# A rotary-embedding kernel on one core: tile t takes batches t, t+4, t+8 and t+12 in place of four neighbouring ones

## The chip, the core and the metric

The kernel runs on one core of a Trainium2 chip. The time is the device time of one launch in microseconds (us); the figure for the kernel before is the median of three runs. The work of this kernel lies on two resources: VectorE (DVE in the profile), which does all the arithmetic, and the 16 DMA engines of the core, which carry every tile from DRAM into SBUF and back. SyncE (SP) and GpSimd (POOL) do nothing here but start transfers. In this document one of the 16 DMA engines is called a lane.

## The reference: what is computed

The input x has 16 batches, 512 positions, 16 heads and 64 values, all float32 (33.55 MB); cos and sin are 512 x 32. Of each 64 values the first 32 are rotated in two quarters of 16, and the last 32 are passed on.

```python
x1, x2 = (x[..., :half_dim].copy(), x[..., half_dim:].copy())
...
rotated_first = x1[..., :half_dim // 2] * cos[..., :half_dim // 2] - x1[..., half_dim // 2:] * sin[..., :half_dim // 2]
rotated_second = x1[..., :half_dim // 2] * sin[..., :half_dim // 2] + x1[..., half_dim // 2:] * cos[..., :half_dim // 2]
return np.concatenate([rotated_first, rotated_second, x2], axis=-1)
```

All batches use the same cos and sin rows, so which batches share a tile does not matter to the arithmetic.

## The kernel before

**Tiles.** The 16 x 512 = 8192 positions are cut into T = 4 tiles. A tile is 128 partitions (P) of K = 16 positions each; a position is R = 1024 floats (16 heads x 64), so one partition's row is 16 x 1024 x 4 B = 64 KB and a tile is 8.39 MB. One batch of 512 positions takes PB = 32 partitions, so a tile holds four batches, one in each group of 32 partitions. Before the change a tile is one contiguous stretch of DRAM: row p of tile t starts at (128 t + p) x 64 KB.

**Buffers.** `ring` (line 45) has NS = 3 places in SBUF; tile t lives in place t % 3, so tile 3 uses the place of tile 0 again. The arithmetic is done in place, and the store reads the same buffer.

**Transfers.** `load` (line 54) and `store` (line 57) are one DMA each: 128 rows of 64 KB, or of 32 KB where tile 2 is loaded in two halves (KC = 8 positions each). On SP's queue stand, in this order: load 0, load 1, the first half of load 2 (lines 65 to 67); then store 0, the second half of load 2, load 3 (lines 107 to 109); then store 1 (line 112) and store 3 (line 126). Store 2 alone is started by POOL (line 116), after the small loads of cos and sin (lines 63 and 64). Load 3 must wait until store 0 has read the place that both use. Store 1 is held back by hand until the middle of tile 2's rotation: lines 118 to 123 make it wait for `near`, the rotation of positions 8 to 12 of tile 2, which itself waits for the second half of load 2.

**Arithmetic.** `rotate` (line 90) is four VectorE instructions for half a tile: two products and two sums (lines 96, 97, 98 and 101). Before the first of them, lines 73 to 86 spread cos and sin over the four groups of 32 partitions.

**What the change touches.** Only the two DRAM views `xf` and `of` (lines 36 and 37) and the indexing of them in `load` and `store`.

Of the kernel before, what the change touches and what calls it, by code (L numbers as in the profile page):

```python
# [1 line left out]

# [4 lines left out]


@with_exitstack
def kernel(  # L10
    ctx: ExitStack,
    tc: tile.TileContext,
    x: bass.AP,
    cos: bass.AP,
    sin: bass.AP,
    out: bass.AP,
):
    nc = tc.nc
    fp32 = mybir.dt.float32
    P = 128  # L20
    B, S, H, D = x.shape
    Q = D // 4
    HF = D // 2

    K = 16
    T = B * S // (P * K)
    PB = S // K
    REP = P // PB  # L30
    R = H * D
    NS = 3
    KC = K // 2
    KM = 13

    xf = x.rearrange("b s h d -> (b s h d)").rearrange("(t p f) -> t p f", t=T, p=P)
    of = out.rearrange("b s h d -> (b s h d)").rearrange("(t p f) -> t p f", t=T, p=P)
    cosf = cos.rearrange("(p k) j -> p (k j)", k=K)
    sinf = sin.rearrange("(p k) j -> p (k j)", k=K)

    const_pool = ctx.enter_context(tc.tile_pool(name="const", bufs=1))
    b_pool = ctx.enter_context(tc.tile_pool(name="bp", bufs=1, space=bass.MemoryType.PSUM))


    ring = const_pool.tile([P, NS, K, H, D], fp32)
    stage = const_pool.tile([P, 2, K, HF], fp32)
    spun = const_pool.tile([P, 2 * K, Q], fp32)
    packed = const_pool.tile([PB, 2 * K, Q], fp32)
    table = const_pool.tile([P, 2, K, 2, Q], fp32)

    def rows(t, lo, hi):
        return ring[:, t % NS, lo:hi].rearrange("p k h d -> p (k h d)")

    def load(t, lo=0, hi=K):
        return nc.sync.dma_start(out=rows(t, lo, hi), in_=xf[t, :, lo * R : hi * R])

    def store(t, lo=0, hi=K, queue=nc.sync):
        return queue.dma_start(out=of[t, :, lo * R : hi * R], in_=rows(t, lo, hi))  # L58


    nc.vector.memset(stage[:, :, :, 0:Q], 0.0)  # L61
    spread = stage.rearrange("(j b) t k i -> j b t (k i)", b=REP)
    nc.gpsimd.dma_start(out=spread[:, 0, 0], in_=cosf)  # L63
    nc.gpsimd.dma_start(out=spread[:, 0, 1], in_=sinf)  # L64
    load(0)
    load(1)
    load(2, 0, KC)

    PQ = PB // REP
    nc.vector.stream_shuffle(  # L73
        out=spun[:],
        in_=stage.rearrange("p t k j -> p (t k) j")[:, :, 0:Q],
        mask=[j % PQ * REP for j in range(PB)],
    )
    for q in reversed(range(REP)):
        n = PQ * (q + 1)
        nc.vector.tensor_copy(out=packed[0:n], in_=spun[q * PB : q * PB + n])  # L80

    for r in range(REP):
        nc.vector.tensor_copy(  # L83
            out=table[r * PB : (r + 1) * PB].rearrange("p t k c j -> p (t k) c j"),
            in_=packed.unsqueeze(2).to_broadcast((PB, 2 * K, 2, Q)),
        )
    C = table[:, 0].rearrange("p k c j -> p k (c j)")
    Sn = table[:, 1].rearrange("p k c j -> p k (c j)")

    def rotate(t, lo, hi):  # L90
        x1 = ring[:, t % NS, lo:hi, :, 0:HF]
        c = C[:, lo:hi].unsqueeze(2).to_broadcast((P, hi - lo, H, HF))
        s = Sn[:, lo:hi].unsqueeze(2).to_broadcast((P, hi - lo, H, HF))
        b_full = b_pool.tile([P, KC, H, HF], fp32, name="b_t")
        b_t = b_full[:, 0 : hi - lo]
        nc.vector.tensor_mul(out=b_t, in0=x1, in1=s)  # L96
        nc.vector.tensor_mul(out=x1, in0=x1, in1=c)  # L97
        nc.vector.tensor_sub(  # L98
            out=x1[:, :, :, 0:Q], in0=x1[:, :, :, 0:Q], in1=b_t[:, :, :, Q:HF]
        )  # L100
        return nc.vector.tensor_add(  # L101
            out=x1[:, :, :, Q:HF], in0=x1[:, :, :, Q:HF], in1=b_t[:, :, :, 0:Q]
        )

    rotate(0, 0, KC)
    rotate(0, KC, K)
    store(0)
    load(2, KC, K)
    load(3)
    rotate(1, 0, KC)  # L110
    rotate(1, KC, K)
    behind_loads = store(1)
    rotate(2, 0, KC)
    near = rotate(2, KC, KM)
    rotate(2, KM, K)
    store(2, queue=nc.gpsimd)

    tc.add_manual_dep(
        behind_loads.ins,
        near.ins.name,  # L120
        mybir.DependencyInfo(mybir.DependencyClass.Sync, mybir.DependencyReason.DATA),
        reason="the store follows the loads at the DMA engines",
    )
    rotate(3, 0, KC)
    rotate(3, KC, K)
    store(3)


# [1 line left out]
_INS = ['x', 'cos', 'sin']  # L130
_OUTS = [((16, 512, 16, 64), 'float32')]


# [23 lines left out]
```

## Time and profile before

| quantity | value |
|---|---|
| median of three runs | 161.63 us (161.45 to 161.63) |
| span of the profiled execution | 159.5 us |
| VectorE busy | 112.9 us in 47 instructions |
| one `rotate` of half a tile (lines 96, 97, 98, 101) | 4.43 + 4.42 + 2.29 + 2.28 us |
| first VectorE instruction on x / end of the last one | 22.99 us / about 131.2 us |
| first row of x moving / last row of the output landed | 1.74 us / 158.2 us |
| packets of 64 KB, and the time of most of them | 896; 2.418 us |
| packets of 32 KB, and the time of most of them | 256; 1.213 us |

The span is the time from the first to the last instruction of one profiled execution; the measured time of a run is some 2.1 us longer. A packet is what one lane carries in one piece; its time runs on that lane. Here each row of a tile is one packet. VectorE's last rotation ends 28 us before the span does: what follows it is the last store. The profile gives "share of 16 engines' span" for each DMA queue: the time of its packets added up and divided by 16 times the span.

### The profile page before, as it was taken

What the parts mean: (1) busy time and instruction counts of PE and PEld (TensorE: products, weight loads), DVE (VectorE), ACT (ScalarE), POOL (GpSimd) and SP (SyncE); (2) the same over time, 40 slices, a digit from 0 to 9 for tenths busy, and PEclk for the clock granted to TensorE, in tenths of its full rate; (3) what the DMA queues carried; (4) which work ended last, traced back from release to release, by engine and by line L of the source; (5) the groups of instructions that cost most, each with busy time, mean ns of one, the idle gap of its engine ahead of it and who ended that gap; (6) DMA issues with size and microseconds to landing.
All of it is one profiled execution on the core that took longest, in us unless ns stands there. A gap on an engine that the chain in (4) does not pass through costs nothing.

```text
span 159.5 us, 115 instructions
## 1 busy us (share of the span) xinstructions
DVE 112.9 (71%) x47; POOL 1.9 (1%) x7
## 2 busy tenths in 40 slices
DVE  1000959999999999999999999999999990000000
POOL 3000000000000000000000000010000000000000
DMA  7969979899699699699996996996996996998966
GB/s 263 542 263 542 444 345 526 362 427 526 271 493 551 263 526 526 263 395 427 493 526 263 526 526 263 526 526 263 526 526 263 526 510 279 526 427 362 526 263 263
DMA packets 1360, 67.24 MB, mean 422 GB/s; under 512 B 176, under 2 KB 176, under 8 KB 208
## 3 DMA queue, kind: packets, MB, share of 16 engines
q1 hardware_dynamic: 1152, 58.72, 85.7%
q0 software_dynamic: 208, 8.52, 12.4%
HBM read 33.69 MB, written 33.55 MB: 422 GB/s over the span
## 4 chain that ended last, share of the span: by engine, by line
DVE 61%; DMA 14%; issue 5%; DVEq 1%
DVE b_t L96 22%; DVE ring L97 22%; DMA ring<-in_x_dram 14%; DVE ring L101 10%; DVE ring L98 7%; DVEq L152 1%; DVEq L96 0%
## 5 line engine op out<-in xcount | busy, mean ns | idle before, releaser
L96 DVE TENSOR_TENSOR b_t<-ring,table 128x4096 f32<-128x4096 f32 (+2 forms) x9 | 35.6, 3959 | 2.1 <-DMA ring<-in_x_dram 1.9
L97 DVE TENSOR_TENSOR ring<-ring,table 128x4096 f32<-128x4096 f32 (+2 forms) x9 | 35.6, 3950 | 0.3
L98 DVE TENSOR_TENSOR ring<-ring,b_t 128x2048 f32<-128x2048 f32 (+2 forms) x9 | 18.4, 2050 | 0.3
L101 DVE TENSOR_TENSOR ring<-ring,b_t 128x2048 f32<-128x2048 f32 (+2 forms) x9 | 18.4, 2043 | 0.0
L73 DVE LOAD_MASK_SELECT spun<-stage x1 | 0.0, 14 | 14.4 <-DMA stage<-in_sin_dram 14.4
L83 DVE COPY table<-packed 32x1024 f32<-32x1024 f32 x4 | 2.7, 684 | 0.1
L58 POOL DMA_DIRECT2D out_dram<-ring x1 | 0.6, 559 | 101.7 <-DVE ring L101 101.7
L80 DVE COPY packed<-spun 32x512 f32<-32x512 f32 (+3 forms) x4 | 1.7, 416 | 0.1
L61 DVE MEMSET stage<- 128x512 f32 x1 | 0.5, 485 | 0.9 <-PEq L141 0.9
L73 DVE STREAM_SHUFFLE spun<-stage 128x512 f32<-128x512 f32 x1 | 0.7, 722 | 0.0
L63 POOL DMA_DIRECT2D stage<-in_cos_dram x1 | 0.6, 642 | 1.3 <-DVE stage L61 1.3
L64 POOL DMA_DIRECT2D stage<-in_sin_dram x1 | 0.5, 532 | 0.0
L141 POOL MEMSET const-bfloat16-1.0<- 128x1 bf16 x1 | 0.1, 101 | 0.0
L141 POOL MEMSET const-float32-0.0<- 128x1 f32 x1 | 0.1, 98 | 0.2 <-issue 0.2
L141 POOL MEMSET const-float32-1.0<- 128x1 f32 x1 | 0.1, 98 | 0.0
L141 POOL MEMSET const-uint8-127<- 128x1 uint8 x1 | 0.1, 98 | 0.0
## 6 DMA issues: line engine op xcount, KB each, us to landing
ring<-in_x_dram SPq DMA_DIRECT2D x2, 4096.0 KB, 40.7
stage<-in_cos_dram POOLq DMA_DIRECT2D x1, 64.0 KB, 8.9
stage<-in_sin_dram POOLq DMA_DIRECT2D x1, 64.0 KB, 13.3
ring<-in_x_dram SPq DMA_DIRECT2D x3, 28.9
out_dram<-ring SPq DMA_DIRECT2D x3, 27.4
out_dram<-ring POOLq DMA_DIRECT2D x1, 39.5
```

The source lines that it names most:

```text
L58: return queue.dma_start(out=of[t, :, lo * R : hi * R], in_=rows(t, lo, hi))
L61: nc.vector.memset(stage[:, :, :, 0:Q], 0.0)
L63: nc.gpsimd.dma_start(out=spread[:, 0, 0], in_=cosf)
L64: nc.gpsimd.dma_start(out=spread[:, 0, 1], in_=sinf)
L73: nc.vector.stream_shuffle(out=spun[:], in_=stage.rearrange("p t k j -> p (t k) j")[:, :, 0:Q], mask=[j % PQ * REP for j in range(PB)],)
L80: nc.vector.tensor_copy(out=packed[0:n], in_=spun[q * PB : q * PB + n])
L83: nc.vector.tensor_copy(out=table[r * PB : (r + 1) * PB].rearrange("p t k c j -> p (t k) c j"), in_=packed.unsqueeze(2).to_broadcast((PB, ...
L96: nc.vector.tensor_mul(out=b_t, in0=x1, in1=s)
L97: nc.vector.tensor_mul(out=x1, in0=x1, in1=c)
L98: nc.vector.tensor_sub(out=x1[:, :, :, 0:Q], in0=x1[:, :, :, 0:Q], in1=b_t[:, :, :, Q:HF])
L101: return nc.vector.tensor_add(out=x1[:, :, :, Q:HF], in0=x1[:, :, :, Q:HF], in1=b_t[:, :, :, 0:Q])
L152: with _tile.TileContext(nc) as tc:
```

## The change

The two DRAM views are built from the batch dimension (g t) instead of from one flat stretch: t is the inner of the two, so tile t has g = 0 to 3 at batches t, t+4, t+8 and t+12. One batch is 2 MB, so the four groups of 32 partitions of one tile are 8 MB apart in DRAM, where they were 2 MB apart. Rows stay 64 KB long and 64 KB apart within a group, and partition 32 g + j still holds positions 16 j to 16 j + 15 of its batch, so the cos and sin tables fit as before.

```diff
-    xf = x.rearrange("b s h d -> (b s h d)").rearrange("(t p f) -> t p f", t=T, p=P)
-    of = out.rearrange("b s h d -> (b s h d)").rearrange("(t p f) -> t p f", t=T, p=P)
+    xf = x.rearrange("(g t) (j k) h d -> t g j (k h d)", t=T, k=K)
+    of = out.rearrange("(g t) (j k) h d -> t g j (k h d)", t=T, k=K)
...
-        return nc.sync.dma_start(out=rows(t, lo, hi), in_=xf[t, :, lo * R : hi * R])
+        return nc.sync.dma_start(out=rows(t, lo, hi), in_=xf[t, :, :, lo * R : hi * R])
...
-        return queue.dma_start(out=of[t, :, lo * R : hi * R], in_=rows(t, lo, hi))
+        return queue.dma_start(out=of[t, :, :, lo * R : hi * R], in_=rows(t, lo, hi))
```

The DRAM side of a transfer thus has three dimensions, 4 x 32 x 16384, where it had two, 128 x 16384. The SBUF side keeps 128 partitions. In the built program the instructions of every engine stand in the same order as before, with the same waits; only the shapes in the nine large transfers differ (here SP's queue; the shape is that of the destination):

```
-L55 DMACopy ring<-in_x_dram 128x16384 x2
-L55 DMACopy ring<-in_x_dram 128x8192
-L58 DMACopy out_dram<-ring 128x16384
+L55 DMACopy ring<-in_x_dram 128x1x16384 x2
+L55 DMACopy ring<-in_x_dram 128x1x8192
+L58 DMACopy out_dram<-ring 4x32x16384
```

## The prediction

> **What bounds the kernel now.** I read the head of the page, its slices and its DMA queues first, then the DMA shares of three windows, then the waits of SP's queue, and last the chain.
>
> ```profile
> span 159.5 us, 115 instructions
> ...
> DVE 112.9 (71%) x47; POOL 1.9 (1%) x7
> ...
> DVE  1000959999999999999999999999999990000000
> ...
> DMA  7969979899699699699996996996996996998966
> ...
> DMA packets 1360, 67.24 MB, mean 422 GB/s; under 512 B 176, under 2 KB 176, under 8 KB 208
> ...
> q1 hardware_dynamic: 1152, 58.72, 85.7%
> q0 software_dynamic: 208, 8.52, 12.4%
> HBM read 33.69 MB, written 33.55 MB: 422 GB/s over the span
> ```
>
> VectorE is idle at both ends, the lanes never are: 85.7 + 12.4 = 98.1% of 16 lanes' time is packets. So the lanes set the end. In numbers: 98.1% of 16 x 159.5 us is 2503 us of lane time for 67.24 MB, 26.9 GB/s a lane. The packet records say it more sharply: of 896 packets of 64 KB nearly all took 2.418 us (27.1 GB/s), loads and stores alike, the 32 KB ones 1.213 us; 16 packets were in flight for 150.7 us, one on each lane. The windows show the same rate in the loads' stretch, in the mixed one and in the last store:
>
> ```profile
> core 0: us, DVE busy (x) POOL busy (x), PEclk, DMA share, GB/s
> 4.00:20.00 16.00, 4.01 (x9) 0.00 (x0) 1.00 1.04 451
> 72.00:99.00 27.00, 26.72 (x12) 0.00 (x0) 1.00 1.03 447
> 140.00:157.00 17.00, 0.00 (x0) 0.00 (x0) 1.00 1.00 432
> ```
>
> (A packet is counted where it starts, hence shares a little over 1.) The small packets tell how a transfer is dealt out: 176 under 512 B is 11 transfers x 16, one closing packet per lane and transfer; q1's 1152 is 8 transfers x 16 plus 5 loads' and 3 stores' 1024 rows. So now all 16 lanes take part in every transfer, 8 rows of 128 each.
>
> ```profile
> SPq L58 <- DVE ring L101: 84.1, 3, 30.5
> ...
> SPq L55 <- DMA out_dram<-ring: 21.0, 1, 21.0
> ```
>
> SP waits long, but the lanes have queued rows meanwhile; those waits cost nothing. The chain of waits names VectorE for most of the span:
>
> ```profile
> DVE 61%; DMA 14%; issue 5%; DVEq 1%
> ```
>
> It runs by semaphores and does not see rows queued on a lane; its DVE share is no sign that VectorE binds. A lower bound of the kernel is the rows' lane time: (896 x 2.418 + 256 x 1.213) / 16 = 154.8 us; 4.7 us of the span are the start (1.74 us before the first row), the slower first rows (2.9 to 3.45 us) and the tail.
>
> **The change, part by part.** *Arithmetic and order:* nothing. The same instructions stand on VectorE, with the same waits; 0 us. *Starting a transfer:* each large transfer has one dimension more. SP's issues took 0.34 us (stores) and 0.43 us (loads), POOL's of the same size 0.56 us. A form that costs as much as POOL's adds 0.2 us on each of eight SP issues; one that is simpler to set up costs nothing or saves as much. Only the first lies ahead of the first row, the others behind queued rows: 0 to 0.2 us, I take 0. *DRAM addresses:* groups lie 8 MB apart, not 2 MB. Every row now takes 2.418 us wherever it lies, so nearer or farther apart there is no time to win but the 1.2 us per lane that slow packets lost above 2.418 us; below that no gain. As a loss I know no row; it stays under the next term, since fewer rows move at once.
>
> *How the rows are dealt to lanes* is the large term. All eleven transfers of the trace have a count of 128 or 32 as outermost dimension on both sides, and all used 16 lanes. Now the nine large ones have an outermost count of 4 on the DRAM side and 128 on the SBUF side. The trace has no such transfer, so I bound it. Low end: rows are dealt by the SBUF side as now, 16 lanes, change 0. High end: one lane for each of the four outer pieces, 32 rows each. A transfer then takes 32 x 2.418 = 77.4 us instead of 8 x 2.418 = 19.3 us. I take four lanes: in every transfer of the trace a lane got whole indices of the outermost dimension (128 / 16 = 8, and 16 closing packets also for the 32 rows of cos), and of 4 there are only four to give.
>
> [...]
>
> *What the four lanes do to each other.* Lane 1 walks partitions 0 to 31, lane 2 partitions 32 to 63, and so on, in step. Low end: each runs its 2.418 us per row, as now where 16 lanes run side by side: eight whole transfers x 77.4 = 619 us. High end: the lanes meet in pairs at one path, and each row takes twice as long, 4.836 us: eight x 154.8 = 1238 us. The nearest row for streams that meet is q0 with q1: store 2 took 39.5 us to land against 27.4 us for q1's, since two streams on a lane take turns and nothing of it overlaps:
>
> ```profile
> out_dram<-ring SPq DMA_DIRECT2D x3, 27.4
> out_dram<-ring POOLq DMA_DIRECT2D x1, 39.5
> ```
>
> Also, a load's row and a store's row take the same 2.418 us though DRAM is read in one and written in the other, so the 27.1 GB/s are set by what both share, lane or SBUF's side; before, each lane had its own eight partitions, so the two were never told apart. I take the high end: lanes started within 0.43 us of each other stay in step, so whatever they share they share all the time.
>
> [...]
>
> *The schedule with T = 154.8 us a transfer.* Loads 0, 1 and half of 2 are queued at once and end at 2.5 T; store 0 is queued after tile 0's rotation (27 us, hidden under load 1) and runs to 3.5 T, half of load 2 to 4 T, load 3 (which waits for store 0, landed half a T earlier) to 5 T. Store 2 goes by POOL's queue from about 4 T on and takes turns with load 3; both end by 6 T; store 1, queued meanwhile, runs to 7 T, and store 3, whose rotation took 27 us under store 1, to 8 T. The lanes are never without rows; all of VectorE's 112.9 us lies under them. If that cover were gone, it would cost a tile's 27 us at most at the end. Sum: 8 T = 1238, + 4.7 for start and tail = 1243 us of span, + 2.1 us (161.6 - 159.5, what a run has around the span) = 1245 us against the median of 161.63.
>
> **The rivals.**
> *Four lanes at full rate.* For it: 2.418 us never changed with what else was moving. Against: no row there had lanes on each other's partitions. 619 + 4.7 + 2.1 = 626 us (own range 610 to 660).
> *Something between.* Lanes fall out of step and meet only in part of the rows (650 to 1200 us), or POOL's store 2 uses four other lanes than SP's: then SP's lanes carry seven transfers, 7 x 154.8 + 6.8 = 1090 us, or 549 at full rate. For it: POOL's transfers have their own queue. Against: in the trace q0 and q1 used the same lanes, and rows kept in step.
> *The other side: still 16 lanes, dealt by the SBUF side.* One mechanism, deciding as soon as the count of lanes is 16: then only addresses differ. For it: the SBUF side still has 128 partitions. Against: a lane would have to take a part of an outermost index, which no transfer of the trace shows. It gives 161.6 us less at most the 1.2 us that slow packets cost now: 160.4 to 161.8 us, not slower. Then the change would do nothing to the time.
>
> **How the numbers follow.** Pairs in step (1200 to 1260 us): 0.58. Four lanes at full rate (610 to 660): 0.22. Between (660 to 1200): 0.10. Store 2 apart at full rate (549): 0.03. Sixteen lanes: 0.07, of which 0.03 faster, 0.02 the same and 0.02 slower by the issue cost. The predicted time is that of the first, 1245 us. It holds 0.58 alone, so the range must take in the full-rate case: 605 to 1265 us, with 0.9 inside. About 0.2%, 0.3 us, is what a measurement here can tell from no change. Slower: 0.58 + 0.22 + 0.10 + 0.03 + 0.02 = 0.95; the same 0.02; faster 0.03.
>
> **What would show it.** Four lanes: DMA share of about 25% of 16 engines over the whole span, 4 in place of 16 closing packets for each of q1's transfers (q1's count 1056 in place of 1152), VectorE idle for four fifths of the span or more. Pairs: rows of 64 KB at about 4.84 us and some 54 GB/s; full rate: 2.42 us and 108 GB/s. A whole load landing about 155 us (77 us) after the first. Store 2 on other lanes: share above 25% while it runs. Wrong altogether: a DMA line of 7s to 9s as before, and 16 packets in flight.

## The result and the profile after

The changed kernel took 884.53 us (median of six runs, 867.69 to 893.85) against 161.63 us before: 5.38 times as long, 95% interval 5.369 to 5.388. That ratio is taken over the faster runs of the six alone; over their median it would be 5.47. The forecast of 1245 us, slower, had the direction and both causes, four lanes and pairs of them at one path; the time lies between its first two cases, since the pairs did not stay in step.

The head of the page, the slices and the queues of the changed kernel:

```profile
span 868.8 us, 115 instructions
...
DVE 112.9 (13%) x47; POOL 2.1 (0%) x7
...
DVE  0200000560000065150000006000001910000000
...
DMA  2222222222222222222222222222222222222220
GB/s 57 58 51 57 51 54 57 54 57 57 60 57 63 60 71 84 77 69 69 72 71 89 104 100 86 106 109 106 103 100 100 106 97 81 84 94 91 97 97 39
DMA packets 1648, 67.24 MB, mean 77 GB/s; under 512 B 464, under 2 KB 464, under 8 KB 496
...
q1 hardware_dynamic: 1056, 58.72, 22.2%
q0 software_dynamic: 592, 8.52, 2.5%
```

VectorE does the same 112.9 us of work. The DMA line is the new thing: a flat row of 2s where 6s to 9s stood, 22.2 + 2.5 = 24.7% of 16 lanes, that is four lanes that are never idle and twelve that carry no row of a tile. q1's packets fell from 1152 to 1056: 1024 rows and 4 closing packets for each of eight transfers. The GB/s line says the rest: about 55 in the first third, over 100 in the middle, and down and up again in the last third. The same bytes, the same four busy lanes, and two rates. The windows put numbers on it (length, busy times, clock, DMA share, GB/s):

```profile
core 0: us, DVE busy (x) POOL busy (x), PEclk, DMA share, GB/s
25.00:150.00 125.00, 5.13 (x10) 0.00 (x0) 1.00 0.25 55
170.00:300.00 130.00, 18.23 (x7) 0.00 (x0) 1.00 0.25 59
560.00:660.00 100.00, 0.00 (x0) 0.00 (x0) 1.00 0.25 104
725.00:860.00 135.00, 0.00 (x0) 0.00 (x0) 1.00 0.24 88
```

What waits now is VectorE, for the loads, and SP, for store 0 before load 3; store 2, which takes turns with load 3, lands after 169.8 us:

```profile
DVE b_t L96 <- DMA ring<-in_x_dram: 556.4, 5, 145.2
```

```profile
SPq L55 <- DMA out_dram<-ring: 190.8, 1, 190.8
```

```profile
out_dram<-ring POOLq DMA_DIRECT2D x1, 169.8
```

In the packet records most rows of 64 KB are of two kinds: 423 of 896 under 2.5 us, as before, and 321 over 4 us, most of them 4.8 to 5.13 us; the 152 between took the slow rate in part. The account of a lane is then simple, as a mean over the four and by the time at which a row starts. Rows at the old speed would fill 619.3 us of each of the four lanes. Above that they lost, per lane: 80.2 us by 161 us (load 0), 66.3 by 310 (load 1), 16.0 by 366 (half of load 2), 30.5 by 455 (store 0), 7.2 by 525 (the other half), 9.9 by 671 (load 3 beside store 2), 6.1 by 725 and 18.7 in the last stores: 234.9 us. 619.3 + 234.9 is 854.2 us of the 865.4 between the first row and the last landing; the lanes did not all end at the same time.

The pattern inside a lane shows what a slow row meets. These are the times, in us, at which the two lanes of one pair begin each group of four rows of load 0 and load 1 (the records do not name lanes; rows are strung together by one's end and the next one's start):

```
first lane   41.46  60.85  79.99  98.91  117.57  135.99  154.10  172.04  189.78
second lane  42.09  61.80  81.11  100.19 119.01  137.59  155.84  173.93  191.84
behind by     0.64   0.95   1.12    1.28    1.44    1.60    1.74    1.89    2.06
```

On the first lane three rows of a group take 4.9 to 5.04 us, and one row at the boundary is shorter, and shorter each time (4.29, 4.10, 3.93, 3.74, 3.56 us): there the first lane has gone on to the next four partitions and the second has not followed yet. On the second lane the first and the last row of a group are both shorter (4.43 and 4.66 us beside 5.00 in the group from 81.11 us). Every fourth row; so the thing they share seems to belong to four neighbouring partitions (half_stagger, below, tests it). And the first lane gains about 0.3 us in the first group shown and about 0.16 us in each later one: they slide out of step.

### The profile page after: what moved, and what is told of

Its sections match the earlier page's. It is cut to its first block, busy times and chain, and to the rows that moved or that the text cites. A ratio compares the mean times of both kernels' runs of the same rounds, so it can differ in the third digit from the quotient of the medians.

```text
span 868.8 us, 115 instructions
## 1 busy us (share of the span) xinstructions
DVE 112.9 (13%) x47; POOL 2.1 (0%) x7
## 3 DMA queue, kind: packets, MB, share of 16 engines
q1 hardware_dynamic: 1056, 58.72, 22.2%
## 4 chain that ended last, share of the span: by engine, by line
another core or an unknown queue 64%; DVE 13%; DMA 3%; DVEq 0%; issue 0%; POOL 0%
DVE b_t L96 4%; DVE ring L97 4%; DMA stage<-in_sin_dram 3%; DVE ring L98 2%; DVE ring L101 2%; DVE table L83 0%; DVEq L152 0%; DVE packed L80 0%; DVE spun L73 0%; POOL stage L63 0%; DVE stage L61 0%; DVEq L96 0%; DVEq L73 0%
## 6 DMA issues: line engine op xcount, KB each, us to landing
out_dram<-ring POOLq DMA_DIRECT2D x1, 169.8
```

## The experiments

The expectations call the explanation to be tested theory A: the outermost count 4 leaves four lanes; lanes whose partitions are 32 apart share a path per four partitions and halve each other while they are in step; the distance in DRAM costs nothing.

**16 lanes with groups 8 MB apart (far16).** The views go back to two dimensions, with the tile's index inside the row's:

```diff
-    xf = x.rearrange("(g t) (j k) h d -> t g j (k h d)", t=T, k=K)
+    xf = x.rearrange("b s h d -> (b s h d)").rearrange("(p t f) -> t p f", t=T, p=P)
```

> Sixteen lanes, groups of 32 partitions 8 MB apart in DRAM: row p of tile t is row 4p + t of x, so neighbouring partitions are 256 KB apart and the transfer keeps two dimensions, 128 x 16384. The rotation then uses cos and sin rows of other positions. Theory A (the outermost count of 4 leaves four lanes, distance in DRAM is harmless): 161.6 us within 0.5 us, rows at 2.418 us, 16 closing packets a transfer. Rival B (the 8 MB distance itself slows the rows): far over 200 us, rows well over 2.418 us.

Measured: 161.6 us, ratio to the kernel before 1.0007 (0.9996 to 1.0018).

```profile
span 159.5 us, 115 instructions
...
DMA packets 1360, 67.24 MB, mean 422 GB/s; under 512 B 176, under 2 KB 176, under 8 KB 208
```

All 176 closing packets are back, and no time is lost or won. The 8 MB did nothing here; rival B falls.

**Four lanes, 4 MB apart (apart4).** The counterpart: another distance, the same shape. (With neighbouring batches, 2 MB apart, the 128 rows are evenly spaced in DRAM and the view becomes 128 x 16384 in the built program, so there is no three-dimensional transfer at 2 MB.)

```diff
+    xf = x.rearrange("(a g b) (j k) h d -> a b g j (k h d)", a=2, b=2, k=K)
...
+        return nc.sync.dma_start(out=rows(t, lo, hi), in_=xf[t // 2, t % 2, :, :, lo * R : hi * R])
```

> Four lanes, groups 4 MB apart in place of 8 MB: tiles hold batches 0,2,4,6 / 1,3,5,7 / 8,10,12,14 / 9,11,13,15. Theory A: like the changed kernel, 850 to 910 us, rows starting at 4.1 to 5.1 us. Rival B (distance): another time, nearer to 626 us, and other row times at the start.

Measured: 891.81 us in one run, inside the changed kernel's own spread, with rows of 4.3 to 5.13 us at the start. The shape does it, at either distance.

**Two lanes that never meet (two_groups).** Two groups of two batches each, so an outermost count of 2 and 64 partitions per lane.

```diff
+    xf = x.rearrange("(g t b) (j k) h d -> t g (b j) (k h d)", g=2, t=T, k=K)
```

> Outermost count 2 in place of 4: two lanes, one for partitions 0 to 63 and one for 64 to 127, groups 16 MB apart. Theory A with paths shared by partitions p and p + 32: the two lanes never meet, every row at 2.418 us from the first to the last, 8 x 64 x 2.418 + 7 = 1245 us. Rival C (rows are slow at first because few lanes work or because the lanes' rows are far apart, whatever partitions they go to): rows of 4 to 5 us at the start as with four lanes, 1400 us or more.

Measured: 1243.74 us. Not one row of 64 KB over 3.69 us, 893 of 896 under 2.5 us. The two lanes ran 0.40 us apart, 16 MB from each other in DRAM: going in step costs nothing by itself. The first load's stretch:

```profile
5.00:150.00 145.00, 5.13 (x10) 0.00 (x0) 1.00 0.13 54
```

Two lanes moved 54 GB/s, as much as the changed kernel's four did from 25 to 150 us (55): two of its four were worth nothing while they were in step.

**Two lanes that always meet (two_by_two).** Again two lanes with 64 rows a tile each, but 32 partitions apart: the changed kernel's transfers in two halves.

```diff
+        for h in range(2):
+            i = nc.sync.dma_start(
+                out=rows(t, lo, hi)[64 * h : 64 * h + 64],
+                in_=xf[t, 2 * h : 2 * h + 2, :, lo * R : hi * R],
+            )
```

(and so in `store`.)

> Two lanes again, but each transfer of the changed kernel cut in two: partitions 0 to 63 and 64 to 127, each with outermost count 2. The two lanes then always are 32 partitions apart; 64 rows a lane and tile as with outermost count 2 for the whole tile. Theory A: rows at 4.5 to 5.1 us at the start, faster as the lanes fall out of step, 1350 to 1750 us. Rival C (count of lanes alone): 1245 us, like the two lanes 64 partitions apart.

Measured: 1455.86 us. The same stretch:

```profile
5.00:150.00 145.00, 5.13 (x10) 0.00 (x0) 1.00 0.12 27
```

27 GB/s is one lane's rate (64 KB in 2.418 us), on two busy lanes. With the same number of lanes and rows, partitions 64 apart ran at full speed (54 GB/s) and partitions 32 apart at half of it. Rival C, that the count of lanes alone matters, falls. In total the loss was smaller than the first stretch says, because these lanes slid apart too (after 1100 us all rows but one took under 2.5 us), and because POOL's store went partly over other lanes (see the last section).

**16 lanes that meet in pairs (sixteen_groups).** An outermost count of 16, eight partitions per lane.

```diff
+    xf = x.rearrange("g (t j k) h d -> t g j (k h d)", t=T, k=K)
```

> Outermost count 16: group g is batch g, partitions 8g to 8g + 7, tile t holds positions 128 t to 128 t + 127 of every batch. The rotation then uses cos and sin rows of other positions. All 16 lanes work, each on eight neighbouring partitions, so that lanes g and g + 4 are 32 partitions apart. Theory A with shared paths: 16 in flight, rows at 4.5 to 5.1 us at the start, 250 to 320 us. Rival C (only the count of lanes matters): 161.6 us, rows at 2.418 us.

Measured: 296.56 us, with 16 packets in flight for some 260 of them. From 5 to 75 us, this kernel and, below it, the kernel before:

```profile
5.00:75.00 70.00, 31.82 (x18) 0.00 (x0) 1.00 1.02 212
```

```profile
5.00:75.00 70.00, 56.77 (x26) 0.00 (x0) 1.00 1.00 431
```

All lanes busy in both, and half the bytes. The DMA share alone would not have told them apart.

**One transfer per group (by_group).** The changed kernel's placement with 16 lanes: four transfers of 32 rows per tile.

```diff
+        for g in range(REP):
+            i = nc.sync.dma_start(
+                out=rows(t, lo, hi)[PB * g : PB * g + PB],
+                in_=xf[t, g, :, lo * R : hi * R],
+            )
```

> The changed kernel's placement with four transfers per tile, one for each group of 32 partitions: outermost count 32 on both sides, so 16 lanes of two rows each; lanes then go two by two to partitions four of which lie side by side. Theory A with paths shared by four neighbouring partitions as well: rows near 4.8 us, 250 to 330 us. Rival C (16 lanes are enough): 162 to 175 us.

Measured: 293.55 us, again 212 GB/s from 5 to 75 us with every lane busy. 660 of its 896 rows of 64 KB took over 4 us. Each lane has two rows of a transfer, so two lanes go to each four neighbouring partitions, and theory A has them meet there. Splitting brings the lanes back but not the speed: of the shapes tried here only the two-dimensional one over all 128 partitions kept both.

**Lanes started out of step (stagger).** Two copies that keep some lanes busy for a while ahead of load 0, and nothing else changed:

```diff
+    junk = nc.dram_tensor("junk", (68, 32768), fp32, kind="Internal").ap()
+    src = x.rearrange("b (s k) h d -> (b s) (k h d)", k=K)
+    nc.sync.dma_start(out=junk[0:17, 0:4096], in_=src[0:17, 0:4096])
+    nc.sync.dma_start(out=junk[17:68, 0:4096], in_=src[17:68, 0:4096])
     load(0)
```

> [...] Theory A (lanes in a pair meet at one path only while they are in step): rows of load 0 and load 1 at 2.418 us from the start, load 0 landed before 115 us in place of 161, in all 640 to 760 us. Rival D (rows get faster with time for another reason, whatever the lanes' step): load 0 at 161 us or later, 880 us in all.

How far the copies put the lanes of a pair apart was my estimate: by a share of 17 rows of 16 KB, which at the 27.1 GB/s of a lane before takes 10.3 us, a little over four rows of 2.418 us. Which lanes carried the copies no run shows.

Measured: 692.26 us (670.71 to 723.17 in six runs), although it moves 1.1 MB more. VectorE's first instructions on load 0 and load 1, in the changed kernel and, below, in this one:

```profile
161.51 4.43 DVE L96 TENSOR_TENSOR b_t<-ring,table 128x4096 f32<-128x4096 f32 x1 [127.93 <-DMA ring<-in_x_dram]
310.74 4.43 DVE L96 TENSOR_TENSOR b_t<-ring,table 128x4096 f32<-128x4096 f32 x1 [122.37 <-DMA ring<-in_x_dram]
```

```profile
101.96 4.43 DVE L100 TENSOR_TENSOR b_t<-ring,table 128x4096 f32<-128x4096 f32 x1 [87.65 <-DMA ring<-in_x_dram]
179.28 4.43 DVE L100 TENSOR_TENSOR b_t<-ring,table 128x4096 f32<-128x4096 f32 x1 [50.46 <-DMA ring<-in_x_dram]
```

The windows of the profiled execution, with a span of 721.2 us:

```profile
25.00:125.00 100.00, 22.87 (x7) 0.00 (x0) 1.00 0.25 106
125.00:340.00 215.00, 48.84 (x16) 0.00 (x0) 1.00 0.25 109
340.00:520.00 180.00, 35.58 (x15) 0.72 (x1) 1.00 0.25 100
520.00:680.00 160.00, 0.00 (x0) 0.00 (x0) 1.00 0.24 78
```

Full speed from the start (106 GB/s from 25 to 125 us, against 55 from 25 to 150 us in the changed kernel), so step it is, and not time: rival D falls. But after store 2 had taken turns with load 3, slow rows came back (78 GB/s from 520 to 680 us).

**The same without turns (stagger_sp).** Store 2 moves to SP's queue:

```diff
-    store(2, queue=nc.gpsimd)
+    store(2)
```

> The staggered kernel with store 2 on SP's queue behind store 1 in place of POOL's. With store 2 on a queue of its own its rows took turns with load 3's, and from some 520 us on rows of 4 to 5.3 us came back. Theory A (two streams on a lane shift the pairs' step; without them the step stays): rows at 2.418 us to the end, 619 us of rows + about 21 us of stagger + 7 us = 645 to 665 us, with less spread from run to run than the 670.7 to 723.2 us of the staggered kernel. Rival F (lanes slide back together with time anyway): 670 to 725 us again, rows over 4 us in the last stores.

Measured: 647.58 us, all four runs from 647.22 to 647.68.

```profile
350.00:640.00 290.00, 26.69 (x8) 0.00 (x0) 1.00 0.24 106
```

No row of 64 KB took over 3.64 us, 887 of 896 took under 2.5 us; per lane 1.3 us were lost above 2.418 us a row, where the changed kernel lost 234.9. The step that the copies set, by the estimate a little over four rows, stayed to the end here; in stagger, with store 2 as a second stream beside load 3, it did not. (Store 2 on SP's queue without the copies was not run.)

**Half a step (half_stagger).** The rows of the two copies cut to 8 KB (`0:2048`).

> The staggered kernel with rows of 8 KB in place of 16 KB in the two small copies: the lanes of a pair start some 5.2 us apart, a little over two rows, half of what the full stagger gave. Theory A with a path that belongs to four neighbouring partitions: in each four rows about half of the time is shared, four rows take about (8 - 2.15) x 2.418 = 14.1 us at first, load 0 landed at 110 to 130 us, load 1 at 200 to 235 us. Rival E (any unequal start is enough): load 0 landed before 100 us, load 1 before 170 us. Rival G (the path belongs to more than four rows): load 0 after 140 us.

Measured: 804.56 us; load 0 landed at 133.5 us, load 1 at 245.5. Both lie a little over A's bounds and far from those of E; G's bound for load 0 was not reached. The rows of one lane in load 0, one after the other, in us:

```
2.77  2.43  4.94  5.12    2.76  2.43  4.77  5.12    2.76  2.43  4.60  5.04
```

Two rows alone, two rows shared, in fours. A group takes 15.3 us here, and 15.8 at the start of the load, and not the 14.1 that I had written: a shared row costs up to 5.12 us and not 2 x 2.418, and the rows alone at the boundary took up to 2.77. This shorter step did not stay: a group took 14.8 us at the end of load 0.

## Why the prediction was right or wrong

*What binds.* Right: the lanes, before and after; VectorE's 112.9 us stayed covered, and the order and waits of the schedule held (load 3 behind store 0, store 2 beside load 3).

*Starting a transfer.* The term taken at 0 was at its high end, and small. SP took 1.91 us for its first three loads in place of 1.33, and 0.58 us for store 0 in place of 0.35: 0.2 us each. The first row moved at 2.20 us in place of 1.74, 0.46 us later, more than the 0.2 allowed; the other issues lie behind queued rows.

*DRAM distance.* Right: no gain and no loss (far16, ratio 1.0007).

*Four lanes.* Right, and shown by q1's 1056 packets, the 24.7%, and counts of 2 and 16 in the other kernels (a DMA share of 0.13 in two_groups and of 1.02 in sixteen_groups). The trace of before had no outermost count of 4: that it leaves four lanes was my estimate from transfers with counts of 128 and 32. Store 2 went over the same four lanes as SP's transfers, as taken: 4.0 packets in flight while it ran.

*Lanes in pairs.* Right in kind while the lanes are in step: two lanes at one path is what two_groups (54 GB/s, partitions 64 apart), two_by_two (27 GB/s, 32 apart) and sixteen_groups (212 GB/s against 431) show. The trace of before did not: 4.836 us a row, all the time, was a bound put at twice 2.418, and no run shows the 154.8 us that it gives for each of eight transfers; loads 0 and 1 came near it, the other six did not. The row that the forecast drew on, 39.5 us against 27.4 for a store, counts from issue, with the wait in the queue; the reading that holds is 39.5 beside two transfers of 19.3 us, and it shows two streams on one lane, not two lanes at one path. Stores share too: in the changed kernel's last stores rows took up to 5.34 us, against 2.418 alone. The size was a little off: fully shared rows of loads 0 and 1 took 4.8 to 5.13 us, against 4.836. Load 0 ran from 2.2 to 161.5 us, 159.3 against 154.8, and load 1 landed 149.2 us later.

*The step that failed* is the sentence "lanes started within 0.43 us of each other stay in step, so whatever they share they share all the time". They do not: the first lane of a pair gained 0.16 us per four rows. For loads 0 and 1 that was little (load 1 landed at 310.7 us; the forecast had 2 T = 310, which is luck in part: load 0 was too long by dearer rows and load 1 too short by the drift). With the 32 KB rows of tile 2 a group of four is half as long, the lead counted for twice as much, and from there most rows ran alone: none of the 256 rows of loads 0 and 1 took under 2.5 us, of the other 640 rows of 64 KB 423 did. The six transfers after load 1 were priced at 154.8 us each, and the pairing added some 30 us at most to the 77.4 us of any of them. In the account: 619 more by pairing was forecast, 235 came. The stagger kernels show that the step makes this difference: started apart, the same four lanes ran at full rate at once, and with store 2 on SP's queue they did so throughout, 647.58 us, which is the second case's 626 plus some 21 us of stagger.

*The chances.* What came was "something between", priced at 0.10 and with its mechanism named, lanes out of step that meet in part of the rows. The forecast should have asked whether being in step is a state that keeps itself. Nothing in the trace of before could say so. The named time was 41% too long; that the range of 605 to 1265 us holds the result is owed to its spanning two cases far apart, neither of which came.

*Left open.* Why the first lane of a pair gains was not found. It is not in the shared rows, which take the same on both lanes (5.02 us in the pair shown, 5.12 and 5.13 in the other), but at the boundary: from 79.99 us on the first lane's boundary row was 1.07 us shorter than its shared rows, the second lane's two only 0.91 us together. Nor was the spread from run to run explained by a run of its own; that it is 0.46 us with the lanes held apart, and 26 us in the changed kernel, speaks for the step. No version here beats the kernel before: its lanes have 154.8 us of rows in 161.6 us.

## What to carry to other kernels

Look at the outermost dimension of every DMA, as built, before anything else: in every kernel here a DRAM view with a count of 2, 4 or 16 there left that many lanes, and where the lanes set the time, as here, the price without pairing was about 16 divided by it (two lanes: 1243.74 us, 7.7 times; four lanes held out of step: 647.58 us, 4.0 times). Then ask which partitions each lane walks, since in sixteen_groups all lanes were busy (a DMA share of 1.02) and half of them worth nothing (212 GB/s against 431); GB/s beside the DMA share shows it, the share alone does not. Where lanes shared a path here, their step decided (884.53 us in the changed kernel, 647.58 with the lanes held apart); in the changed kernel, apart4, two_by_two and sixteen_groups the time came out between the bound of lanes always in step and that of lanes never in step.

## What the runs showed of the hardware that I had not expected

- In the changed kernel the lanes of a pair left their step by themselves, about 0.16 us per four shared rows, and a shared row of loads 0 and 1 cost up to 6% more than twice a row alone (5.13 us against 4.836).
- On POOL's queue store 2 over few lanes brought small packets, as many as one for each row on each lane that it did not use (the records do not name lanes): q0 had 592 packets in place of 208 in the changed kernel, 384 = 12 lanes x 32 rows more, and 1104 with two lanes, 896 = 14 x 64 more. In two_groups, which has the 896, the time was 1243.74 us, against the 1245 expected without them.
- One of POOL's two transfers in two_by_two went over other lanes than SP's; the records do not say which. From 900 to 1050 us 0.24 of 16 lanes were busy, where two lanes are 0.13:

```profile
900.00:1050.00 150.00, 13.89 (x8) 1.37 (x2) 1.00 0.24 76
```

- In the changed kernel POOL's only transfer on four lanes shared SP's (4.0 packets in flight while it ran). Which lanes POOL's queue takes next was not tried further.
